# A three-block network on one core: the residual's update at the end of the hybrid mixer, on VectorE alone instead of with GpSimd

## The chip, the core and the metric

The kernel runs on one core of a Trainium2 chip. TensorE does the matrix products and the transposes, VectorE and ScalarE the elementwise work, GpSimd a little of it, and the SyncE queue issues the loads. The metric is the device time of one execution in microseconds.

## What is computed

The input is one sequence of 256 tokens with 1024 columns. It goes through a forgetting-attention layer and a retention layer, each followed by a SwiGLU feed-forward, then a norm, and then through a second block. The second block is the one that matters here:

```python
def second_block(x, ...):
    h = rms_norm(x, attn_pre_norm)
    mix = hybrid_mixer(h, ...)                 # two attentions side by side, then @ w_out
    x = x + rms_norm(mix, attn_post_norm)      # the residual's update
    h = rms_norm(x, ffn_pre_norm)              # the next norm
    f = (silu(h @ w_gate) * (h @ w_up)) @ w_down
    x = x + rms_norm(f, ffn_post_norm)
```

Every number is float32. The large products are made of three products of split numbers: an operand is kept as a high part H and a low part L = x - H.

## The kernel before

The residual lies in one tile `XR` (the profile calls it `xg`, after the tensor that it was loaded into), the tokens on the partitions in two token tiles of 128 at this point of the program. `self.xn(t, hf)` is half `hf` (512 columns) of token tile `t`. The weights come as a stream of granules: `gran` loads one into `raw`, ScalarE makes its high part `wh` (line 221), VectorE its low part `wl` (line 222), and TensorE multiplies. `take` runs up to six granules ahead. A scheduler fixes the order of the instructions on each engine, and each engine works strictly in that order.

The hybrid mixer ends like this. Four heads of the differential attention (`diff_head`: scores on TensorE at lines 1211 and 1212, row maxima with the mask on VectorE at line 1114, exponentials on ScalarE at line 1116) run after the last heads of the other attention (`nsa_head`: transposes at lines 1146 and 1150, values at line 1159). Products of the output projection fill TensorE between them. Then `done(t, banks)` of `post_prep` takes the two PSUM banks of a token tile: `post_norm` squares and sums them on ScalarE (line 318), scales them on VectorE (line 495), and GpSimd raises the sum to the power -1/2 (line 325).

What the next stage needs is `h` transposed and split into `XH` and `XL` (both in the tile `xt`; `split`: H on ScalarE at line 249, L on VectorE at line 250). The kernel before gets it without waiting for the new residual. While the heads still run, GpSimd prepares `xg[t] = X[t] * g` for both token tiles (line 1263, a tile with the same name `xg` in the profile) and `gpg = gp * g` (line 1265), where `gp` is the weight of the norm after the mixer and `g` that of the next norm. Then the split's input is `bank * gpg * r + xg` (lines 495 and 514). The residual itself follows on the side: `add = bank * r * gp` on VectorE (line 516) and `X += add` on GpSimd in `late()` (line 530), after which ScalarE squares it for the next norm (line 318).

The next stage is `ffn` with its first gate chunk (`gate`, Silu on ScalarE at line 616), first for token tile 0 and then for token tile 1; its first products are those of lines 228 to 230, `acc<-wh,xt`.

Of the kernel before, what the change touches and what calls it, by code (L numbers as in the profile page):

```python
# [69 lines left out]
def tiles(w, nk):  # L70
    """w, 1024 rows: granules of nk K tiles each, K on the partitions."""
    return w.reshape(8 // nk, nk, 128, -1).transpose(0, 2, 1, 3).reshape(8 // nk, 128, -1)


def column_tiles(chunks):
    """Granules of 128 x 1024 (or less) of each chunk of columns."""
    out = []
    for parts in chunks:
        w = [m[:, c:c + n] for m, c, n in parts]
        w = np.concatenate(w, axis=1) if len(w) > 1 else w[0]  # L80
        out.append(tiles(w, 4 if w.shape[1] == 256 else 2))
    return np.ascontiguousarray(np.concatenate(out, axis=0))


def row_tiles(w):
    """For each 128 columns of w all its rows, K tile by K tile."""
    return np.ascontiguousarray(w.reshape(-1, 128, 8, 128).transpose(2, 1, 0, 3).reshape(8, 128, -1))


def chunks(w, *cols):  # L90
    """512 columns each from cols; (c,) stands for two chunks of 256."""
    out = []
    for c in cols:
        out += [[(w, c[0], 256)], [(w, c[0] + 256, 256)]] if isinstance(c, tuple) else [[(w, c, 512)]]
    return out


def layout(inputs):
    """The inputs (and constants of the shapes) as the kernel reads them: moved, never computed with."""
# [39 lines left out]
class Net:  # L139
# [48 lines left out]
    def plan(self, src, nk):  # L188
        """Queue granules (nk K tiles each) for take(), in the order of their use."""
        self.queue += [(src[i], nk) for i in range(src.shape[0])]  # L190

    def xn(self, t, hf):
        """The 512 columns hf of token tile t of the residual, while its tokens lie on the partitions."""
        return self.XR[:, 4 * hf:4 * hf + 4, t * 128:(t + 1) * 128]
# [10 lines left out]
    def take(self, hold=0):  # L205
        """The next granule, as (H, L); hold earlier ones are still to be read.  Loads run ahead of it."""
        n = self.taken
        while self.queue and self.made < n - hold + (2 if n < 8 else WBUFS):
            self.ready.append(self.gran(*self.queue.pop(0)))
            self.made += 1  # L210
        self.taken += 1
        return self.ready.pop(0)
# [19 lines left out]
    def run_after(self, fill, then):  # L232
        """then(), its products behind those of the next step of fill, if there is one."""
# [6 lines left out]
    def mm_wide(self, ps, H, L, x, first, last):  # L240
        """ps[:, 0] + ps[:, 1] += H.T @ x[:, 0] + H.T @ x[:, 1] + L.T @ x[:, 0], x = (H, L) side by side."""
# [10 lines left out]
    def xs_part(self, ps, t, i, g):  # L252
        """Adds granule g, two K tiles from 2 i on, of h @ W for the tokens of tile t."""
# [6 lines left out]
    def xs(self, n):  # L260
        """n columns of h @ W, tokens on the partitions: the first token tile as early as it can be."""
# [8 lines left out]
    def xs_steps(self, n, then):  # L270
        """The same granule by granule, for both token tiles; then(t, bank) at the end."""
# [13 lines left out]
    def ws_wide(self, late=False, between=None):  # L285
        """256 columns of h @ W with the columns on the partitions: of each 128 the two addends [128, 2, S]."""
# [12 lines left out]
    def ws(self, between=None):  # L299
        """256 columns of h @ W as two tiles with the columns on the partitions."""  # L300
# [27 lines left out]
    def means(self, acc):  # L328
        """[128, 2] in PSUM: the mean square of each token, for the two token tiles."""
# [11 lines left out]
    def norm(self):  # L341
        """r[t] = 1 / rms of the transposed residual."""
# [5 lines left out]
    def norm_twice(self):  # L348
        """r[t] as of norm() for X = (residual * gf) / rms; returns that 1 / rms, [128, 2]."""
# [14 lines left out]
    def to_rows(self, t, hf, r):  # L364
        """Turns a quarter of the residual, scaled by r, to tokens on the partitions."""
# [5 lines left out]
    def rows(self, cols):  # L371
        """[128, 256] with the two token tiles' columns along every partition."""
# [6 lines left out]
    def out_part(self, bank, g, x, t, hf, first, last):  # L379
        """Adds one K tile, x = (H, L) with K on the partitions, to half hf of the columns of token tile t."""  # L380
# [6 lines left out]
    def out_proj(self, n, lhs, done):  # L387
        """X-side product with K on lhs(k) -> (H, L); done(t, [bank, bank]) takes each token tile."""
# [20 lines left out]
    def out_T(self, nk, lhs, ahead, cut, done):  # L409
        """The residual's transposed update, 128 columns after 128 columns; done(d, bank) takes the two addends  # L410
        of each."""
# [27 lines left out]
    def add_out(self, d, ps):  # L439
        """Adds the update, times scale (one number for each token) if there is one, to the residual."""  # L440
# [10 lines left out]
    def add_T(self, i):  # L451
        """Residual and the split of its norm with the gain i, but for the factor of each token."""
# [17 lines left out]
    def add_norm_T(self, i, f):  # L470
        """The same for a norm with the gain f ahead of it: the residual is left times f."""
# [11 lines left out]
    def post_norm(self, t, banks, g, scaled, f=None):  # L483
        """scaled[hf] = bank * f * g; returns 1 / rms of the rows of the two banks times f."""
# [18 lines left out]
    def post_prep(self, gp, gpg, xg):  # L503
        """X += norm(banks) * gp, and the split of its norm; xg[t] = X[t] * g and gpg = gp * g."""
        nc = self.nc

        def done(t, banks):
            pg = [self.half_tile("pg") for hf in range(2)]
            add = [self.half_tile("add") for hf in range(2)]
            r = self.post_norm(t, banks, gpg, pg)  # L510
            for hf in range(2):
                ks = slice(4 * hf, 4 * hf + 4)
                v = pg[hf].rearrange("p (k n) -> p k n", k=4)
                nc.vector.scalar_tensor_tensor(v, v, r, xg[t][:, ks, :], op0=OP.mult, op1=OP.add)
            for hf in range(2):
                nc.vector.scalar_tensor_tensor(add[hf], banks[hf], r, gp[:, hf * 512:(hf + 1) * 512], op0=OP.mult,
                                               op1=OP.mult)

            def late():
# [8 lines left out]
                for hf in range(2):  # L528
                    x = self.xn(t, hf)
                    nc.gpsimd.tensor_add(x, x, add[hf].rearrange("p (k n) -> p k n", k=4))  # L530
                    self.sumsq(x, a[:, hf:hf + 1])
# [15 lines left out]
    def start_T(self):  # L547
        """The first norm, from x already transposed, and the first chunk of columns."""
# [56 lines left out]
    def ffn(self, done=None, out=None):  # L605
        """done: of the transposed product; out: of the other, the norm's input then being the other as well."""
# [284 lines left out]
    def hybrid(self, gp, gn):  # L891
# [3 lines left out]
        with ExitStack() as st:  # L895
# [23 lines left out]
            def rope(outs, ps, c, s, n):  # L919
                """ps, and each of outs: [128, n, 64] (or [128, a, b, 64])."""  # L920
# [43 lines left out]
            def head_rope_T(t, ps, c, s):  # L964
                """[128 (two heads, d), 4, 128 tokens] of ps, token tile t of 512 columns."""
# [10 lines left out]
            def compressed(i):  # L976
                """The flattened blocks (plus positions), features on the partitions: H and L side by side."""
# [70 lines left out]
            def stack(tr, t):  # L1048
                """Per head H on its own half of the partitions and L on the other half."""
# [126 lines left out]
            def d_evac(i, t, ps):  # L1176
                """Token tile t of the chunk of the differential q, k or v."""
# [82 lines left out]
            xg = []  # L1260
            for t in range(2):
                xg.append(b4("xg", 8, 128))
                nc.gpsimd.tensor_mul(xg[t], self.XR[:, :, t * 128:(t + 1) * 128],
                                     gn.rearrange("p (k n) -> p k n", k=8))
            nc.gpsimd.tensor_mul(gn, gn, gp)
            done = self.post_prep(gp, gn, xg)
# [145 lines left out]
```

## Time and profile before

| | |
|---|---|
| median of three runs | 1050.95 us (1050.90 to 1051.66) |
| span of the profiled execution | 1051.4 us |
| TensorE busy | 1025.1 us, 98% |
| VectorE busy | 739.8 us, 70% |
| ScalarE busy | 568.4 us, 54% |
| GpSimd busy | 32.1 us, 3%, 37 instructions |

The span is that of one execution taken with the profiler, and the three times are of runs without it. They lie around the span, so the time outside the span is no larger than the scatter of the runs. A busy share says how long an engine had work; it does not say whether somebody waited for that work.

### The profile page before, as it was taken

To read this page: it belongs to the slowest core of one execution; us is meant where nothing else is said; L and a number is where in the kernel's file an instruction comes from. 1 tells how busy PE (TensorE), PEld (TensorE's weight loads), DVE (VectorE), ACT (ScalarE), POOL (GpSimd) and SP (SyncE) were. 2 spreads that over 40 slices of the span, in tenths; PEclk is the share of its full clock that TensorE was granted. 3 is DMA by queue.
4 is the path that set the end of the run, shared out by engine and by line. 5 is a ranking of instruction groups with operands and counts; after the bars stand their busy time and mean duration, and the time that the engine had idled before them with its cause. 6 is when DMAs were issued, how large, how long until landed. Compare 5 with 4: busy or idle time off the path is not lost.

```text
span 1051.4 us, 15380 instructions
## 1 busy us (share of the span) xinstructions
PE 1025.1 (98%) x5798; PEld 878.4 (84%) x5798; DVE 739.8 (70%) x1243; ACT 568.4 (54%) x914; POOL 32.1 (3%) x37
## 2 busy tenths in 40 slices
PE   7999999999999999999999999999998989999997
PEld 6999888888889888888888888888776768888885
DVE  6855977676777766767767767778787676776643
ACT  6545666564444354354565655566556655565531
POOL 1000000000000000000000000000003030000000
PEclk9999999999999999999999999999999999999999
DMA  8543755656665455446766566556433046656551
GB/s 273 205 146 116 241 189 181 192 180 184 185 203 178 132 173 186 150 162 199 235 189 184 185 183 190 190 155 216 139 107 101 22 145 215 183 181 197 188 174 40
DMA packets 53386, 181.19 MB, mean 172 GB/s; under 512 B 6833, under 2 KB 8369, under 8 KB 53185
## 3 DMA queue, kind: packets, MB, share of 16 engines
q1 hardware_dynamic: 53280, 180.19, 53.6%
q8 instruction: 45, 0.74, 0.3%
q14 instruction: 29, 0.23, 0.1%
q0 software_dynamic: 32, 0.03, 0.0%
HBM read 179.15 MB, written 1.05 MB: 171 GB/s over the span
## 4 chain that ended last, share of the span: by engine, by line
PE 91%; DVE 3%; DMA 3%; ACT 1%; issue 1%; POOL 1%; DVEq 0%; ACTq 0%; POOLq 0%
PE acc L243 23%; PE acc L244 12%; PE s L243 11%; PE acc L228 10%; PE acc L230 10%; PE acc L229 10%; PE s L244 6%; DVE wl L222 1%; PE o L1159 1%; DMA raw<-in_fox_w_dram 1%; ACT wh L221 1%; DMA raw<-in_hyb_w_dram 1%; PE o L228 1%; PE o L230 1%; PE o L229 1%
## 5 line engine op out<-in xcount | busy, mean ns | idle before, releaser
L222 DVE TENSOR_TENSOR wl<-raw,wh 128x1024 fp32r<-128x1024 f32 (+2 forms) x342 | 410.2, 1203 | 205.1 <-ACT wh L221 204.5
L221 ACT ACTIVATE wh<-raw 128x1024 fp32r<-128x1024 f32 (+2 forms) x342 | 352.3, 1033 | 276.6 <-PE acc L230 61.3
L243 PE MATMUL acc<-xt,wh 128*128 128x512 f32 x496 | 180.7, 398 | 0.0
L243 PE MATMUL s<-xt,wh 128*128 128x512 f32 x496 | 180.6, 397 | 0.0
L244 PE MATMUL acc<-xt,wl 128*128 128x256 f32 x496 | 129.5, 281 | 0.0
L244 PE MATMUL s<-xt,wl 128*128 128x256 f32 x496 | 129.3, 281 | 0.0
L243 PE MATMUL acc<-ht,wh 128*128 128x512 f32 x352 | 122.1, 392 | 0.0
L228 PE MATMUL acc<-wh,xt 128*128 128x512 f32 (+1 forms) x288 | 116.6, 405 | 1.5 <-DVE rm L933 0.9
L230 PE MATMUL acc<-wh,xt 128*128 128x512 f32 (+1 forms) x288 | 115.3, 401 | 2.7 <-DVE xt L250 2.7
L229 PE MATMUL acc<-wl,xt 128*128 128x512 f32 (+1 forms) x288 | 114.0, 396 | 0.0
L243 PEld LDWEIGHTS acc<-xt,wh 128*128 128x128 f32 x496 | 93.3, 188 | 16.8
L243 PEld LDWEIGHTS s<-xt,wh 128*128 128x128 f32 x496 | 93.3, 188 | 16.8
L244 PEld LDWEIGHTS s<-xt,wl 128*128 128x128 f32 x496 | 93.6, 189 | 5.9
L244 PEld LDWEIGHTS acc<-xt,wl 128*128 128x128 f32 x496 | 93.7, 189 | 5.6
L244 PE MATMUL acc<-ht,wl 128*128 128x256 f32 x352 | 96.6, 282 | 0.0
L243 PEld LDWEIGHTS acc<-ht,wh 128*128 128x128 f32 x352 | 65.1, 188 | 13.4
L228 PE MATMUL acc<-xt,wh 128*128 128x256 f32 x256 | 73.2, 286 | 0.0
L230 PE MATMUL acc<-xt,wl 128*128 128x256 f32 x256 | 72.1, 282 | 0.0
L229 PE MATMUL acc<-xt,wh 128*128 128x256 f32 x256 | 72.1, 282 | 0.0
L244 PEld LDWEIGHTS acc<-ht,wl 128*128 128x128 f32 x352 | 66.3, 188 | 1.5
L230 PEld LDWEIGHTS acc<-wh,xt 128*128 128x128 f32 x288 | 55.1, 191 | 14.7 <-DVE xt L250 3.1
L228 PEld LDWEIGHTS acc<-wh,xt 128*128 128x128 f32 x288 | 55.3, 192 | 13.9 <-issue 1.4
(354 smaller groups left out, 1528.9 us busy)
## 6 DMA issues: line engine op xcount, KB each, us to landing
raw<-in_ffn_w_dram SPq DMA_DIRECT2D x132, 512.0 KB, 3.8
raw<-in_ret_w_dram SPq DMA_DIRECT2D x48, 512.0 KB, 3.6
raw<-in_ffn_out_dram SPq DMA_DIRECT2D x32, 512.0 KB, 3.9
raw<-in_w_down_dram SPq DMA_DIRECT2D x22, 512.0 KB, 3.6
raw<-in_fox_w_dram SPq DMA_DIRECT2D x20, 512.0 KB, 4.7
raw<-in_hyb_w_dram SPq DMA_DIRECT2D x20, 512.0 KB, 4.4
raw<-in_ret_out_dram SPq DMA_DIRECT2D x16, 512.0 KB, 4.2
raw<-in_ffn_out_dram SPq DMA_DIRECT2D x16, 384.0 KB, 3.4
```

The costliest lines, as they stand in the source:

```text
L221: nc.scalar.activation(H, w, AF.Copy)
L222: nc.vector.tensor_sub(L, w, H.bitcast(F32))
L228: mm(out, xh, wh, start=first, stop=False, **kw)
L229: mm(out, xh, wl, start=False, stop=False, **kw)
L230: self.last = mm(out, xl, wh, start=False, stop=last, **kw).ins
L243: whole = lambda: mm(ps, H, x, start=first, stop=last).ins
L244: part = lambda: mm(ps[:, 0, :], L, x[:, 0, :], start=False, stop=False).ins
L1159: nc.tensor.matmul(o[hs, t, :], VN[i // 2][:, i % 2, g, :], pt[:, 2 * t + i, :], start=i == 0, stop=i == n - 1)
```

## The change

The residual is updated in place first, `X = (bank * gp) * r + X`, and the split's input is the product `X * g`, both on VectorE. The four products and adds `X += add`, the two products `X[t] * g` and the product `gp * g` on GpSimd are gone, and so are the tiles `xg` and `add`. The square for the next norm is taken of the residual directly. The rest of the diff empties docstrings.

```diff
-    def post_prep(self, gp, gpg, xg):
+    def post_prep(self, gp, g):
         nc = self.nc
 
         def done(t, banks):
             pg = [self.half_tile("pg") for hf in range(2)]
-            add = [self.half_tile("add") for hf in range(2)]
-            r = self.post_norm(t, banks, gpg, pg)
+            r = self.post_norm(t, banks, gp, pg)
             for hf in range(2):
-                ks = slice(4 * hf, 4 * hf + 4)
+                x = self.xn(t, hf)
                 v = pg[hf].rearrange("p (k n) -> p k n", k=4)
-                nc.vector.scalar_tensor_tensor(v, v, r, xg[t][:, ks, :], op0=OP.mult, op1=OP.add)
-            for hf in range(2):
-                nc.vector.scalar_tensor_tensor(add[hf], banks[hf], r, gp[:, hf * 512:(hf + 1) * 512], op0=OP.mult,
-                                               op1=OP.mult)
+                nc.vector.scalar_tensor_tensor(x, v, r, x, op0=OP.mult, op1=OP.add)
+                nc.vector.tensor_mul(v, x, g[:, hf * 512:(hf + 1) * 512].rearrange("p (k n) -> p k n", k=4))
 
             def late():
...
                 for hf in range(2):
-                    x = self.xn(t, hf)
-                    nc.gpsimd.tensor_add(x, x, add[hf].rearrange("p (k n) -> p k n", k=4))
-                    self.sumsq(x, a[:, hf:hf + 1])
+                    self.sumsq(self.xn(t, hf), a[:, hf:hf + 1])
                 self.r[t] = self.rstd(a)
...
-            xg = []
-            for t in range(2):
-                xg.append(b4("xg", 8, 128))
-                nc.gpsimd.tensor_mul(xg[t], self.XR[:, :, t * 128:(t + 1) * 128],
-                                     gn.rearrange("p (k n) -> p k n", k=8))
-            nc.gpsimd.tensor_mul(gn, gn, gp)
-            done = self.post_prep(gp, gn, xg)
+            done = self.post_prep(gp, gn)
```

VectorE's order at the end of the mixer, from the sum of squares of token tile 0 on, before the change (`nv` is the input of the power -1/2, `nf` a factor that only the last norm reads):

```order
L323 SCALAR_TENSOR_TENSOR nv<-na 128x1
L495 TENSOR_TENSOR pg<-acc,gain 128x512
L514 SCALAR_TENSOR_TENSOR pg<-pg,nr,xg 128x512 x2
L516 SCALAR_TENSOR_TENSOR add<-acc,nr,gain 128x512 x2
L222 TENSOR_TENSOR wl<-raw,wh 128x1024 x2
L250 TENSOR_TENSOR xt<-tr,xt 128x4x128 x2
```

and with the change:

```order
L323 SCALAR_TENSOR_TENSOR nv<-na 128x1
L495 TENSOR_TENSOR pg<-acc,gain 128x512
L513 SCALAR_TENSOR_TENSOR xg<-pg,nr,xg 128x4x128 x2
L514 TENSOR_TENSOR pg<-xg,gain 128x512 x2
L222 TENSOR_TENSOR wl<-raw,wh 128x1024 x2
L250 TENSOR_TENSOR xt<-tr,xt 128x4x128 x2
```

There are as many VectorE instructions ahead of the first `xt` as before, but the two that replace `add` now stand between the new residual and the transposes of `pg`. The second token tile has the same exchange.

ScalarE's order from the third granule of the next stage's weights to the first Silu, before the change (the last two lines of `xt` are token tile 1):

```order
L221 ACTIVATE wh<-raw 128x1024
L318 ACTIVATE sq,na<-xg 128x512
L318 ACTIVATE sq,na<-acc 128x512
L318 ACTIVATE sq,na<-s 128x512
L249 ACTIVATE xt<-tr 128x4x128 x2
L318 ACTIVATE sq,na<-xg 128x512
L616 ACT_TABLE_LOAD
L616 ACTIVATE sg<-acc,nr 128x512
```

and with the change:

```order
L221 ACTIVATE wh<-raw 128x1024
L318 ACTIVATE sq,na<-acc 128x512
L221 ACTIVATE wh<-raw 128x1024
L318 ACTIVATE sq,na<-s 128x512
L318 ACTIVATE sq,na<-xg 128x512 x2
L611 ACT_TABLE_LOAD
L611 ACTIVATE sg<-acc,nr 128x512
L249 ACTIVATE xt<-tr 128x4x128 x2
```

The two `xt` of token tile 1 moved behind the table load and the Silu of token tile 0, which read the finished product of token tile 0. On TensorE the eight transposes of token tile 1 moved behind the last product of token tile 0; they stood four products earlier. GpSimd's order only loses the seven instructions, and the order of the loads is unchanged. Up to the end of the heads the order on TensorE, VectorE and ScalarE is the same.

## Rows read from the trace of the kernel before

**Rows 1.** The waits of TensorE over the whole span, two of the longest: who waited for whom, microseconds in total, times, the longest.

```profile
PE s L1211 <- DVE nm L1114: 3.0, 1, 3.0
...
PE acc L230 <- DVE xt L250: 2.7, 1, 2.7
```

**Rows 2.** Two stretches of the span: their length, then busy time (and instructions) of TensorE, its weight loads, VectorE, ScalarE and GpSimd, the granted TensorE clock, the DMA share and GB/s.

```profile
822.00:846.00 24.00, 22.73 (x119) 16.84 (x119) 16.48 (x59) 14.87 (x52) 2.01 (x2) 1.00 0.24 76
867.00:1045.00 178.00, 177.59 (x908) 149.65 (x906) 109.13 (x135) 90.59 (x124) 1.08 (x2) 1.00 0.53 171
```

**Rows 3.** GpSimd's instructions in order of time: start and duration in us (of all merged ones together), line, operation, output and inputs, in brackets the idle time before it and who ended it.

```profile
802.17 4.91 POOL L1263 TENSOR_TENSOR xg<-xg,gain 128x1024 f32<-128x1024 f32 x2 [101.84 <-PE s L1127]
807.16 3.21 POOL L1265 TENSOR_TENSOR gain<-gain 128x1024 f32<-128x1024 f32 x1
...
850.69 3.49 POOL L530 TENSOR_TENSOR xg<-xg,add 128x512 f32<-128x512 f32 x2 [2.19 <-DVE add L516]
```

**Rows 4.** VectorE in order of time among the heads, in the same columns.

```profile
793.81 2.52 DVE L222 TENSOR_TENSOR wl<-raw,wh 128x1024 fp32r<-128x1024 f32 x2
...
803.00 1.84 DVE L250 TENSOR_TENSOR ol<-on,oh 128x256 fp32r<-128x256 f32 x1
804.77 3.39 DVE L222 TENSOR_TENSOR wl<-raw,wh 128x1024 fp32r<-128x1024 f32 x1
...
808.84 1.56 DVE L1138 TENSOR_TENSOR fc<-fc,G 128x4 f32<-128x4 f32 x1
...
813.53 0.16 DVE L1138 TENSOR_TENSOR fc<-fc,G 128x4 f32<-128x4 f32 x1
...
823.43 0.43 DVE L250 TENSOR_TENSOR ol<-on,oh 128x256 fp32r<-128x256 f32 x1 [0.80 <-ACT oh L249]
```

**Rows 5.** TensorE in order of time among the heads. Its matmuls overlap, so the distance of two starts says more than a duration.

```profile
799.90 1.52 PE L1159 MATMUL o<-pt,vn 128*64 128x128 f32 x12
...
805.64 0.39 PE L229 MATMUL acc<-wl,oh 128*128 128x512 f32 x1
809.06 0.46 PE L1211 MATMUL s<-dT 64*128 64x128 f32 x2 [3.03 <-DVE nm L1114]
...
809.88 0.51 PE L230 MATMUL acc<-wh,ol 128*128 128x512 f32 x1
811.35 1.09 PE L1146 MATMUL tr<-c,pr 128*128 128x128 f32 x4 [0.97 <-DVE pr L1139]
...
815.52 2.77 PE L1159 MATMUL o<-pt,vn 128*64 128x128 f32 x12
...
819.88 1.52 PE L1159 MATMUL o<-pt,vn 128*64 128x128 f32 x12
```

**Rows 6.** ScalarE in order of time: the copy of the transposed weights of the last of those heads.

```profile
818.92 0.60 ACT L1147 ACTIVATE pt<-tr 128x512 f32<-128x512 f32 x1 [2.22 <-PE tr L1146]
```

**Rows 7.** Three stretches, in the columns of Rows 2; the number behind the five engines is the granted TensorE clock (1.00 is 2.4 GHz, 0.50 is 1.2 GHz).

```profile
747.00:749.00 2.00, 2.00 (x6) 1.54 (x5) 1.94 (x8) 1.23 (x2) 0.00 (x0) 0.50 0.57 154
814.00:816.00 2.00, 2.00 (x6) 0.98 (x5) 1.52 (x6) 0.78 (x4) 0.00 (x0) 0.50 0.00 0
26.00:28.00 2.00, 2.00 (x19) 2.00 (x18) 0.67 (x2) 2.00 (x3) 0.00 (x0) 1.00 0.87 297
```

**Rows 8.** TensorE at the hand-over from the mixer to the feed-forward: the transposes of `pg` of token tile 0, the first products of the next stage, and two of its products later.

```profile
850.86 1.03 PE L525 MATMUL tr<-c,pg 128*128 128x128 f32 x8
852.48 0.50 PE L228 MATMUL acc<-wh,xt 128*128 128x512 f32 x1 [0.59 <-ACT xt L249]
...
855.92 0.80 PE L230 MATMUL acc<-wh,xt 128*128 128x512 f32 x1 [2.70 <-DVE xt L250]
...
864.38 0.40 PE L230 MATMUL acc<-wh,xt 128*128 128x512 f32 x1
864.62 0.39 PE L228 MATMUL acc<-wh,xt 128*128 128x512 f32 x1
```

**Rows 9.** VectorE at the hand-over, token tile 0.

```profile
848.54 1.41 DVE L514 SCALAR_TENSOR_TENSOR pg<-pg,nr,xg 128x512 f32<-128x512 f32 x2
...
851.19 4.08 DVE L222 TENSOR_TENSOR wl<-raw,wh 128x1024 fp32r<-128x1024 f32 x2
```

**Rows 10.** A VectorE operation of the same kind as the new product (two inputs in SBUF, 512 columns), from the mixer's start: times it occurs, shortest, median and longest duration in ns, first and last start.

```profile
L935 DVE TENSOR_TENSOR nat<-nat,rm x6: 679/684/693, 735.7 to 786.5; 128x512 f32<-128x512 f32 x6
```

**Rows 11.** ScalarE at the hand-over: the high parts of token tile 1 and the first Silu with its table load.

```profile
862.28 1.27 ACT L249 ACTIVATE xt<-tr 128x512 fp32r<-128x512 f32 x2 [5.76 <-PE tr L525]
...
864.17 1.28 ACT L616 ACT_TABLE_LOAD   x1
865.47 0.69 ACT L616 ACTIVATE sg<-acc,nr 128x512 f32<-128x512 f32 x1
```

**Rows 12.** Three stretches at the hand-over, in the columns of Rows 2.

```profile
854.00:856.00 2.00, 0.08 (x1) 0.09 (x1) 2.00 (x3) 1.94 (x6) 0.18 (x1) 0.92 0.69 242
856.00:858.00 2.00, 2.00 (x5) 1.61 (x6) 2.00 (x4) 0.52 (x2) 0.26 (x1) 0.50 0.73 207
858.00:860.00 2.00, 2.00 (x7) 1.54 (x7) 1.95 (x5) 0.00 (x0) 0.83 (x2) 0.73 0.72 160
```

**Rows 13.** TensorE at another wait, earlier in the mixer.

```profile
745.12 0.51 PE L1126 MATMUL s<-KTH,QS 128*128 128x512 f32 x1 [1.84 <-DVE QS L1054]
```

**Rows 14.** TensorE at a wait near the start of the program.

```profile
25.14 0.43 PE L375 MATMUL tr<-c,nr 128*128 128x128 f32 x2 [1.19 <-POOL nr L338]
```

## The prediction

> **What bounds the kernel now.** I read the waits of TensorE first. It is the busiest engine, and two of its three longest waits lie near the change: 3.0 us for a VectorE row-maximum instruction among the heads, and 2.7 us for VectorE's low part at the hand-over to the feed-forward [rows 1]. Then I asked which parts of the span only TensorE paces. From 867 to 1045 us it is busy 177.59 of 178 us, and from 822 to 846 us 22.73 of 24 [rows 2]. What happens earlier only shifts these stretches, so time saved at the two waits should reach the end of the span. Last I read the four engines in order of time around the waits. The reader is to see that both times GpSimd is at work, and that the VectorE instruction ahead of the wait is slow just then.
>
> **Among the heads: what the removed GpSimd products cost.** GpSimd works on its three products from 802.17 to 807.08 and from 807.16 to 810.37 [rows 3]. In that time three VectorE instructions are slow [rows 4]: a low part of 256 columns takes 1.84 us (0.43 later), a weight's low part 3.39 (1.26 as the mean of two before), and a product on 4 columns 1.56 (0.16 later). That last one ends at 810.40, when GpSimd ends. The excess is 1.41 + 2.13 + 1.40 = 4.94 us. GpSimd is idle for long before and after, and I take its work to be the cause. The Trainium skill, SBUF — State Buffer, "Who interferes with whom", says the same of a VectorE instruction with two SBUF inputs beside a GpSimd one that reads SBUF: the later of the two is held up entirely until the other is done. By that rule GpSimd's products also cost VectorE whole waits rather than a share of speed; the trace agrees in the 1.56 us.
>
> Step one is the 3.03 us wait. TensorE's last product before it starts at 805.64 and the next at 809.06 [rows 5]. Products of this size start 0.23 us apart (864.38 and 864.62 [rows 8]), so it could go on at 805.87. The row maximum that it waits for stands behind the first two slow instructions, so it comes 3.5 us sooner, near 805.4. That is early enough: TensorE gains 809.06 - 805.87 = 3.2 us.
>
> Step two is the wait at 811.35, of 0.97 us, for a product that stands behind all three slow instructions. It ends 4.9 us sooner, near 806.3. TensorE comes there 0.82 + 0.23 = 1.05 us after its start at 809.06 (809.88 is the last product between [rows 5]), which is now 806.9. The gain so far is 811.35 - 806.9 = 4.4 us.
>
> Step three is the clock. After the long idle stretch TensorE runs at 1.2 GHz, 0.50 in the stretch from 814 to 816 [rows 7]. Twelve value products take 2.77 us there and 1.52 at the full clock [rows 5], a factor of 0.55. From 811.35 to the last head's value products at 819.88 it needs 8.53 us; 0.55 of this is 4.7. ScalarE must still copy the transposes: 0.60 us for the first copy, and 0.96 us from its start to the products [rows 6, 5]. I lay the transposes' end at 810.85, and the products at 811.75 instead of 819.88. If the idle stretch is gone, I expect the full clock. Steps one to three then give **8.1 us**. The bounds: 4.4 if the clock falls nevertheless, 8.5 if nothing waits at all, and nothing if GpSimd was not the cause. I take 8.1 because the full clock holds from 822 to 846 with the same kinds of work and two short waits [rows 2].
>
> **At the hand-over, token tile 0.** VectorE's four instructions ahead of the weights' low parts are two of the old kind, 1.41 us, and two that I exchange [rows 9]: `add` from PSUM is replaced by a product with both inputs in SBUF. The nearest row for it is 684 ns [rows 10], against 0.7 us each for the ones removed; the strided output of the in-place update has no row, and I set it at nothing (at most 0.1 us, since the old one reads strided operands elsewhere at the same speed). The weights' low parts begin at 851.1 instead of 851.19. There they take 4.08 us for two [rows 9] while GpSimd adds from 850.69 to 854.18 [rows 3]. Without GpSimd two take 2.4 to 2.5 us (2.52 [rows 4]). TensorE goes on 0.65 us after their end (855.27 to 855.92 [rows 8, 9]), so at 854.05 instead of 855.92: 1.9 us sooner. The longer way to the transposes is hidden: the second product ends near 851.2, and TensorE, busy with the other token tile until 850.86, reaches the second four of its eight transposes (1.03 us together) near 851.4 [rows 8].
>
> **At the hand-over, token tile 1: a new wait.** In the new order ScalarE does the table load and the Silu of token tile 0 before the high parts of token tile 1, and the Silu needs the whole product of tile 0. Behind those high parts stands TensorE's first product of tile 1, and behind it the stage. From 854.05 there are 22 products of 0.23 to 0.24 us, to 859.2, then eight transposes to about 860.6 (VectorE's product for the second four is ready near 860.0). ScalarE has finished the squares near 859.55; 1.28 us of table load, 0.6 for the Silu and 0.6 for the first high part [rows 11] end at 862.05. TensorE idles about 1.45 us here, where it had no wait before. Four products later is the one that started at 864.38 [rows 8]; it now starts near 863.0. So of the 1.9 us **1.4** are left. Bounds: 1.9 if the wait is hidden, and a loss of 1.8 if the clock falls twice (below).
>
> **The rest costs nothing.** Weight loads keep their order; they are freed by VectorE's and ScalarE's work, which comes earlier too. The 0.5 us power on GpSimd stays.
>
> **Sum.** 8.1 + 1.4 = 9.5 us. The profiled execution's 1051.4 becomes 1041.9. The median of the runs is 0.45 below that span, so I forecast **1041.5 us**.
>
> **The rivals.**
>
> *The clock falls at the hand-over.* Two idle stretches remain there, about 1.2 us (852.85 to 854.05) and 1.45 us. The rows around waits of that size disagree: after 1.84 us [rows 13] the clock is 0.50 from 747 on [rows 7], after 1.19 us near the start [rows 14] it stays at 1.00 from 26 on [rows 7]. Before the change the hand-over ran 0.32 + 2 + 1.08 = 3.4 us at half the clock (shares 0.92, 0.50, 0.73 [rows 12]), which is 1.7 us lost. A fall at tile 0 delays the end of its product and with it the Silu, so it takes all of the 1.4 and 0.2 more: 1043.1 us. A second one at tile 1 adds 1.7: 1044.8. Both waits are nearer to 1.19 than to 1.84, so I forecast no fall. The Trainium skill, TensorE: Matmul & The Clock Gate, "A second HAM failure mode: psum-queue depth-cycling", speaks for this rival: short, repeated idling between groups of products is enough to make the clock go down and up again. By that rule it falls at both places, 1044.8 us.
>
> *Among the heads the clock stays down.* Only the 4.4 us come: with 1.4 this is 1045.1 us. Against it: no wait of any size is left there.
>
> *The slow VectorE instructions have another cause.* Then nothing changes among the heads. The hand-over's slow pair would have it too, and only the new wait is left: between 1050 and 1051 us, no change. The coincidence of three starts and ends with GpSimd's speaks against it. The same time comes out if a weight load takes the shift back between 822 and 1045; against it, TensorE has next to no idle time there.
>
> *Slower: the new wait at token tile 1.* If ScalarE came to the high parts of tile 1 later than I think, every microsecond is one of TensorE's. The kernel as a whole gets slower by over 0.2% only from a wait of 1.45 + 9.5 + 2.1 = 13 us on, or, if the heads return nothing, of 5 us: 1053 us. In front of the high parts stand 1.28 + 0.69 us of known work, and the product that this waits for ends before the transposes that TensorE does anyway. That is far from either.
>
> **How the numbers follow.** Forecast 0.50; the clock falls at the hand-over 0.30; it stays down among the heads 0.10; no gain among the heads or the shift taken back 0.07; slower 0.03. The range takes in the first three: low 1040.2 (8.5 and 1.9 with some tenths for the starts), high 1045.5. Runs of this kernel differ by 0.07%, and 0.2% (2.1 us) is about what a measurement can tell from no change. The first three cases are faster by more than that: 0.90; same 0.07; slower 0.03.
>
> **What would show it.** Right: the wait on line 1114's result among the heads is gone, low parts of 1024 columns take 1.2 us there, the clock is 1.00 from 805 to 820 on the old scale, and the head's last value products come 8 us sooner. At the hand-over the two low parts take 2.5 us, TensorE's wait for L250 is about 1.2 us, and a new wait of about 1.5 us stands behind the Silu. Wrong: 0.50 in any stretch there, a VectorE instruction that is slow without GpSimd, or the shift of 822 not found at 1045.

## The result and the profile after

The changed kernel takes **1041.02 us** (median of four, 1039.83 to 1042.91). The kernel before takes 1051.31 (median of four) beside it on the same chip. The ratio is 0.9903, with an interval of [0.9889, 0.9918]: 8.6 to 11.7 us are gained. The forecast was 1041.5 in a range of 1040.2 to 1045.5, and the measured time lies in it. The span of the profiled execution is 1039.6 us, its own time 1041.37.

Every run gives its time and its span. In the runs of the kernel before, 2.5 us of the time lie outside the span (59 runs, 2.46 to 2.59), in those of the changed kernel 1.8 (9 runs, 1.74 to 1.83). So about 0.7 of the 10.3 us gained lie outside the span, and no run here shows why. The sentence ahead of the prediction that the time outside the span is no larger than the scatter does not hold: the profiled execution of 1051.4 us was a long one, and two later ones of the same kernel have spans of 1049.3 and 1048.9.

The engines' busy time on the page:

```profile
PE 1022.5 (98%) x5798; PEld 876.8 (84%) x5798; DVE 733.0 (71%) x1243; ACT 568.6 (55%) x914; POOL 19.8 (2%) x30
```

TensorE's longest waits, in the columns of [rows 1]:

```profile
PE s L568 <- DVE fs L250: 5.4, 1, 5.4
PE acc L228 <- ACT xt L249: 1.8, 2, 1.5
PE acc L230 <- DVE xt L250: 1.2, 1, 1.2
```

The 3.0 us for the row maximum are gone, the 2.7 us for VectorE's low part have become 1.2, and a wait of 1.5 us for ScalarE's high part is new. L568 belongs to the start of the program. Line numbers are smaller than before: L1109, L1133, L1154 and L1206 are now what L1114, L1138, L1159 and L1211 were.

VectorE among the heads, the three instructions of [rows 4]:

```profile
800.27 0.42 DVE L250 TENSOR_TENSOR ol<-on,oh 128x256 fp32r<-128x256 f32 x1
800.61 1.22 DVE L222 TENSOR_TENSOR wl<-raw,wh 128x1024 fp32r<-128x1024 f32 x1
...
802.50 0.16 DVE L1133 TENSOR_TENSOR fc<-fc,G 128x4 f32<-128x4 f32 x1
```

TensorE in the same place (to [rows 5]):

```profile
798.62 0.50 PE L1122 MATMUL s<-KTL,QS 128*128 128x512 f32 x1
...
803.23 0.49 PE L1206 MATMUL s<-dT 64*128 64x128 f32 x2
...
804.42 0.60 PE L1141 MATMUL tr<-c,pr 128*128 128x128 f32 x4
...
809.79 1.52 PE L1154 MATMUL o<-pt,vn 128*64 128x128 f32 x12
```

The stretch that answers to 814 to 816 of [rows 7]:

```profile
804.00:806.00 2.00, 2.00 (x12) 1.37 (x11) 0.74 (x8) 1.43 (x5) 0.00 (x0) 1.00 0.40 154
```

The slow three of 1.84, 3.39 and 1.56 us take 0.42, 1.22 and 0.16. TensorE goes through without a wait, at 2.4 GHz (granted clock 1.00).

TensorE at the hand-over (to [rows 8]):

```profile
840.77 1.07 PE L522 MATMUL tr<-c,pg 128*128 128x128 f32 x8
842.05 0.50 PE L228 MATMUL acc<-wh,xt 128*128 128x512 f32 x1 [0.22 <-ACT xt L249]
...
843.99 0.50 PE L230 MATMUL acc<-wh,xt 128*128 128x512 f32 x1 [1.21 <-DVE xt L250]
...
849.23 1.22 PE L522 MATMUL tr<-c,pg 128*128 128x128 f32 x8
852.00 0.50 PE L228 MATMUL acc<-wh,xt 128*128 128x512 f32 x1 [1.54 <-ACT xt L249]
...
853.04 0.40 PE L230 MATMUL acc<-wh,xt 128*128 128x512 f32 x1
```

VectorE's low parts of the weights (to [rows 9]) and ScalarE ahead of tile 1 (to [rows 11]):

```profile
840.98 2.36 DVE L222 TENSOR_TENSOR wl<-raw,wh 128x1024 fp32r<-128x1024 f32 x2
...
849.47 1.28 ACT L611 ACT_TABLE_LOAD   x1
850.77 0.69 ACT L611 ACTIVATE sg<-acc,nr 128x512 f32<-128x512 f32 x1
851.35 1.08 ACT L249 ACTIVATE xt<-tr 128x512 fp32r<-128x512 f32 x2
```

The two stretches in which TensorE idled (to [rows 12]):

```profile
842.00:844.00 2.00, 0.74 (x3) 0.31 (x3) 2.00 (x4) 2.00 (x6) 0.00 (x0) 1.00 0.44 41
850.00:852.00 2.00, 0.46 (x5) 0.22 (x3) 1.13 (x4) 1.99 (x4) 1.29 (x1) 1.00 0.41 94
```

Both waits are there, about as long as forecast (1.2 and 1.45), and the clock keeps its 1.00 through both.

**Where the span went.** Four marks cut the span so that kernels can be compared stretch by stretch: TensorE's first L1122 product among the heads (L1127 before), the value products of the last of those heads, the last Silu of the feed-forward, and TensorE's last product. The rows of before that stand for the first, third and fourth:

```profile
801.35 0.50 PE L1127 MATMUL s<-KTL,QS 128*128 128x512 f32 x1
...
979.55 0.63 ACT L645 ACTIVATE sg<-sg 128x512 f32<-128x512 f32 x1 [0.59 <-DVE sg L644]
...
1044.19 0.39 PE L230 MATMUL o<-wh,ht 128*128 128x512 f32 x1
```

All kernels of this study, in us (each stretch from one profiled execution; the time is the median of its own runs). They ran in groups on different chips. The kernel before took 1051.31 beside after, 1050.53 beside e1 to e4, 1052.01 beside a2, e5 and e6, 1050.11 beside e7 and e8, and 1050.16 beside b2 and b3; times of different groups are compared through the ratio to it, which is given with each run:

| kernel | time | start to heads | heads | hand-over to last Silu | to last product |
|---|---|---|---|---|---|
| before | 1051.31 | 801.35 | 18.53 | 159.67 | 64.64 |
| b2_before | 1051.30 | 799.45 | 18.43 | 159.60 | 64.65 |
| b3_before | 1051.42 | 798.31 | 18.94 | 159.78 | 64.66 |
| after | 1041.02 | 798.62 | 11.17 | 158.40 | 64.65 |
| a2_after | 1040.36 | 797.55 | 11.17 | 158.37 | 64.65 |
| e1_products_back | 1048.40 | 797.25 | 18.98 | 158.37 | 64.65 |
| e2_no_products | 1042.15 | 797.84 | 11.16 | 159.83 | 64.65 |
| e3_one_product | 1040.92 | 796.49 | 12.06 | 158.35 | 64.65 |
| e4_gp_memsets | 1040.20 | 798.66 | 11.17 | 158.40 | 64.65 |
| e5_early_silu | 1038.84 | 797.23 | 11.16 | 157.14 | 63.14 |
| e6_order | 1038.54 | 798.84 | 11.16 | 156.40 | 63.14 |
| e7_tile_copy | 1040.47 | 800.30 | 11.16 | 158.40 | 63.14 |
| e8_silu_no_tile | 1038.60 | 798.38 | 11.17 | 157.08 | 64.65 |

From before to after the heads lose 18.53 - 11.17 = 7.36 us and the way from there to the last Silu 159.67 - 158.40 = 1.27, together 8.6. The spans differ by 11.8. Of the rest 2.73 us lie ahead of the heads, where the order of TensorE, VectorE and ScalarE did not change; two runs below are on that.

### The profile page after: what moved, and what is told of

Read it like the earlier page. It is cut to its first block, busy times and chain, and to the rows that moved or that the text cites. A ratio compares the mean times of both kernels' runs of the same rounds, so it can differ in the third digit from the quotient of the medians.

```text
span 1039.6 us, 15367 instructions
## 1 busy us (share of the span) xinstructions
PE 1022.5 (98%) x5798; PEld 876.8 (84%) x5798; DVE 733.0 (71%) x1243; ACT 568.6 (55%) x914; POOL 19.8 (2%) x30
## 4 chain that ended last, share of the span: by engine, by line
PE 95%; DVE 2%; DMA 1%; ACT 1%; issue 1%; POOL 0%; DVEq 0%; ACTq 0%; POOLq 0%
PE acc L243 23%; PE acc L244 12%; PE s L243 11%; PE acc L228 11%; PE acc L230 11%; PE acc L229 11%; PE s L244 6%; PE o L1154 1%; DVE wl L222 1%; PE o L228 1%; PE o L230 1%; PE o L229 1%; DMA raw<-in_hyb_w_dram 0%; DMA raw<-in_v_w_dram 0%; PE tr L845 0%
```

## The experiments

My theory (Theory 1 in the texts): GpSimd's products, which read SBUF, hold up VectorE instructions with two SBUF inputs. Among the heads this makes two TensorE waits, and behind them the clock falls to half. The hand-over gives a small part of its own.

### The three products put back into the changed kernel

```diff
+            xg = []
+            for t in range(2):
+                xg.append(b4("xg", 8, 128))
+                nc.gpsimd.tensor_mul(xg[t], self.XR[:, :, t * 128:(t + 1) * 128], ...)
+            gpg = self.late.tile([128, DM], F32, name="gpg", bufs=1)
+            nc.gpsimd.tensor_mul(gpg, xg[1].rearrange("p k n -> p (k n)"), gp)
             done = self.post_prep(gp, gn)
```

> The changed kernel with three GpSimd products of the old sizes put back among the heads (two of the residual by the weight, one of the same length after them); nobody reads their results. Theory 1 (GpSimd holds VectorE up there, TensorE waits, its clock falls): the heads lose what they had gained, 7.4 to 8.1 us, so 1048 to 1049.5 us; TensorE again waits about 3 us for line 1109, and the low part of 1024 columns takes about 3.4 us. Theory 2 (the gain among the heads comes from somewhere else: other tiles, weights that arrive at another time): as fast as the changed kernel, 1040 to 1042 us.

Measured: 1048.4 us, ratio to before 0.998 [0.9971, 0.999]. GpSimd's products, VectorE and TensorE in its trace, in order of time:

```profile
798.06 4.91 POOL L1258 TENSOR_TENSOR xg<-xg,gain 128x1024 f32<-128x1024 f32 x2 [99.24 <-PE s L1122]
...
798.90 1.84 DVE L250 TENSOR_TENSOR ol<-on,oh 128x256 fp32r<-128x256 f32 x1
800.66 3.39 DVE L222 TENSOR_TENSOR wl<-raw,wh 128x1024 fp32r<-128x1024 f32 x1
...
804.95 0.77 PE L1206 MATMUL s<-dT 64*128 64x128 f32 x2 [3.03 <-DVE nm L1109]
```

A stretch behind that wait, in the columns of [rows 2]:

```profile
808.00:810.00 2.00, 2.00 (x8) 1.28 (x6) 0.78 (x6) 1.80 (x8) 0.00 (x0) 0.50 0.03 8
```

The products alone bring back the slow instructions to the hundredth of a microsecond, the wait of 3.03 us and the clock of 0.50. They cost 7.8 us in the trace (18.98 against 11.17). In the times it is 8.2 against the kernel with memsets below, which ran beside it (1048.40 and 1040.20). What stays of the gain is 2.1 us (1.1 to 3.0). The hand-over's 1.3 us in the trace and the 0.7 us outside the span (1.8 here too) make up that size.

### The products alone taken out of the kernel before

```diff
-            xg = []
-            for t in range(2):
-                xg.append(b4("xg", 8, 128))
-                nc.gpsimd.tensor_mul(xg[t], ...)
-            nc.gpsimd.tensor_mul(gn, gn, gp)
+            xg = [self.XR[:, :, t * 128:(t + 1) * 128] for t in range(2)]
             done = self.post_prep(gp, gn, xg)
```

> The kernel before with the three GpSimd products among the heads left out: the residual itself stands in for X * g, and the weight g for gp * g, so the outputs lack a factor; every other instruction stays, the GpSimd adds at the hand-over too. Theory 1: 7.4 to 8.1 us faster than before, 1043 to 1044 us; the hand-over keeps its wait of 2.7 us. Theory 2: no change among the heads, 1050 to 1052 us.

Measured: 1042.15 us, ratio 0.9926 [0.9909, 0.9944], so 5.9 to 9.6 us gained. Its hand-over keeps the adds and the `add` tiles of before; TensorE's wait there:

```profile
PE acc L230 <- DVE xt L250: 2.8, 1, 2.8
```

The stretch behind it, with the granted clock of 0.54:

```profile
846.00:848.00 2.00, 2.00 (x7) 1.58 (x6) 2.00 (x5) 0.00 (x0) 0.98 (x2) 0.54 0.66 244
```

The heads are as short as in after (11.16 us). The hand-over shows the long wait of before and the fallen clock, and takes 1.43 us more than in after. So in the traces the two parts of the change add up, and each is seen alone. VectorE's two weight low parts at the hand-over take 4.13 us here beside GpSimd's adds, 4.08 before and 2.36 in after. But no run took the adds alone away and left VectorE's order as it was, so at the hand-over the adds as the cause are argued from the same pattern and not shown.

### One product of the three, or GpSimd work that only writes

The first run keeps the first product alone:

```diff
+            xg = b4("xg", 8, 128)
+            nc.gpsimd.tensor_mul(xg, self.XR[:, :, 0:128], gn.rearrange("p (k n) -> p k n", k=8))
             done = self.post_prep(gp, gn)
```

> The changed kernel with only the first of the three GpSimd products put back, its result unread. It holds up one VectorE instruction by 1.4 us, of which 0.5 us are hidden behind TensorE's products. If the price is a wait plus a fall of the clock that only a long wait brings: 0.9 us slower than the changed kernel, about 1042, clock 1.00 among the heads. If the price is in proportion to GpSimd's work: about 2.6 us, 1043.6.

The second puts eight memsets of 128x1024 in the products' place, so that GpSimd is as long at work but reads nothing:

```diff
+            for t in range(2):
+                xg = b4("xg", 8, 128)
+                for i in range(4):
+                    nc.gpsimd.memset(xg, float(i))
             done = self.post_prep(gp, gn)
```

> The changed kernel with eight GpSimd memsets of 1024 columns in the place of the products, about 8 us of GpSimd that writes SBUF and reads nothing. If only GpSimd's reads stand in VectorE's way (the Trainium skill, SBUF - State Buffer, says so of a VectorE instruction with two inputs in SBUF): no VectorE instruction is slower, 1040 to 1042 us as the changed kernel. If any GpSimd work there holds VectorE up: 1048 to 1049.5 us.

Measured: 1040.92 us (0.9907 [0.9891, 0.9922]) with one product, 1040.2 us (0.9901 [0.9885, 0.9918]) with the memsets. The one product beside VectorE and TensorE:

```profile
797.30 2.39 POOL L1256 TENSOR_TENSOR xg<-xg,gain 128x1024 f32<-128x1024 f32 x1 [97.74 <-PE s L1122]
...
798.14 1.84 DVE L250 TENSOR_TENSOR ol<-on,oh 128x256 fp32r<-128x256 f32 x1
799.90 1.21 DVE L222 TENSOR_TENSOR wl<-raw,wh 128x1024 fp32r<-128x1024 f32 x1
...
802.01 0.46 PE L1206 MATMUL s<-dT 64*128 64x128 f32 x2 [0.85 <-DVE fc L1133]
```

The memsets beside the same two VectorE instructions:

```profile
799.46 7.45 POOL L1258 MEMSET xg<- 128x1024 f32 x8 [99.61 <-PE s L1122]
...
800.31 0.42 DVE L250 TENSOR_TENSOR ol<-on,oh 128x256 fp32r<-128x256 f32 x1
800.65 1.22 DVE L222 TENSOR_TENSOR wl<-raw,wh 128x1024 fp32r<-128x1024 f32 x1
```

One product holds up one VectorE instruction, until it ends at 799.69; the next one runs at full speed. TensorE waits 0.85 us, keeps its clock, and loses 12.06 - 11.17 = 0.9 us. A third of GpSimd's work costs an eighth of the 7.4 us, so the price is not in proportion to GpSimd's time: it sits in the length of TensorE's wait and in the clock. The timed median cannot tell 0.9 us from nothing, so this rests on the trace.

The memsets keep GpSimd busy for 7.45 us and cost VectorE nothing. The Trainium skill, SBUF — State Buffer, "Who interferes with whom", says that a VectorE instruction with two SBUF inputs contends with GpSimd instructions that read SBUF, and not with those that only write. The two runs agree with both halves (1.84 us beside a product, 0.42 beside memsets).

### The new wait at the hand-over: an early Silu, and another order

Three kernels ran beside each other on one chip: the changed kernel again, one with a small Silu ahead of the last differential norm, so that ScalarE loads its table there, and that one with three weight granules moved behind the work that TensorE waits for.

> The changed kernel once more, as the yardstick for the two kernels beside it: 1041.0 us, 10 us under the kernel before. Among the heads TensorE should again show no wait on VectorE's row maximum, with 11.2 us from the product of the first L1122 there to the last L1154. The 2.7 us by which the changed kernel's profiled execution came earlier to the heads already is, by my theory, an accident of a weight load in the execution of before and no part of the change: then this execution may show a wait of some 1.8 us ahead of the heads (as before did at 745), or none, with the same distances behind it. If it were of the change, the heads would again begin 2.7 us earlier than in the kernel before.

Measured: 1040.36 us, 0.9896 [0.9881, 0.991]. Same heads, same hand-over (table above). It came to the heads at 797.55 us with no wait for `QS` ahead of them, which leaves both readings open; two runs of the kernel before, further down, go on from there.

```diff
                 nc.vector.tensor_scalar(a, a, EPS, None, op0=OP.add)
+                if last:
+                    nc.scalar.activation(self.sm.tile([128, 1], F32, name="early"), a[:, 0:1], AF.Silu)
...
```

The lines that are cut pass `last`, which is true for the second of the two norms.

> The changed kernel with one small Silu more, of 128x1, ahead of the last differential-attention norm, so that ScalarE loads its table before the hand-over. Theory (TensorE's new wait of 1.54 us before tile 1's first product is the table load of 1.28 us on ScalarE's path to the high parts): that wait falls to 0.2 to 0.3 us, the product that started at 853.04 comes 1.3 us sooner, 1039.7 us. If ScalarE waits at that place for the product of tile 0 or for the squares anyway, the wait of 1.5 us stays: 1041 us. If the early load is on the path of the differential norm, it costs up to 1.3 us there: 1041 us too, with the wait at the hand-over gone.

Measured: 1038.84 us, 0.9871 [0.9856, 0.9885]. The table load lies elsewhere, and the wait of 1.54 us is 0.25:

```profile
829.32 1.28 ACT L1243 ACT_TABLE_LOAD   x1
...
849.34 0.50 PE L228 MATMUL acc<-wh,xt 128*128 128x512 f32 x1 [0.25 <-ACT xt L249]
```

That is 1.26 us in the trace (158.40 to 157.14), as expected: the load was on the path of the new wait with its whole length. But the last stretch also fell, from 64.65 to 63.14 us, which no theory had foreseen.

```diff
+        with ExitStack() as st:
+            for ins in self.behind.pop(0) if self.behind else ():
+                st.enter_context(self.tc.issue_after(ins))
             nc.scalar.activation(H, w, AF.Copy)
             nc.vector.tensor_sub(L, w, H.bitcast(F32))
...
+                if not t:
+                    self.behind += [[], [m.ins]]
...
+            if t:
+                self.behind += [[m.ins], [m.ins, self.sq]]
```

Here `m` is the last low part of tile 0's transposes in the first list, and tile 1's product with the gain in the second; `self.sq` is tile 1's last square.

> The kernel of e5 with the order at the hand-over changed too: the low parts of the feed-forward's second granule of weights stand behind the low parts of tile 0's transposes, those of the third and fourth behind tile 1's product with the gain. Theory (the 1.21 us wait of TensorE for tile 0's low parts is VectorE's two weight low parts of 1.2 us each in front of them): that wait falls to some 0.1 us, and tile 1's norm comes up to 1.2 us sooner: together with e5's part 2.0 to 2.6 us under the changed kernel, 1038.4 to 1039.0. Rival (VectorE's and ScalarE's whole work at the hand-over is the bound, whatever its order): TensorE then waits as long a little later, for the weights' low parts that were put back, and the time is that of e5 within 0.4 us.

Measured: 1038.54 us, 0.9868 [0.9854, 0.9882]. What is left of TensorE's waits at the hand-over (L528 are the transposes of tile 1, L530 their high parts):

```profile
PE tr L528 <- DVE pg L518: 0.5, 1, 0.5
...
PE acc L232 <- ACT xt L530: 0.2, 1, 0.2
```

The 1.21 us for tile 0's low part is gone and 0.45 us came back at the transposes of tile 1. The trace shows 0.74 us beyond e5 (157.14 to 156.40), between theory (1.2) and rival (under 0.4). The times of e5 and e6 cannot be told apart.

### What shortened the last stretch

Two kernels separate the early table load from the small tile that its result needs. Their diffs are shown against the kernel of e5.

```diff
-                    nc.scalar.activation(self.sm.tile([128, 1], F32, name="early"), a[:, 0:1], AF.Silu)
+                    nc.scalar.activation(self.sm.tile([128, 1], F32, name="early"), a[:, 0:1], AF.Copy)
```

> The run of the early Silu showed a second gain that nobody had asked for: from the last Silu of the feed-forward to TensorE's last product 63.14 us instead of the 64.65 of six other kernels. This run has the changed kernel with the same small tile of 128x1, but a Copy by ScalarE in place of the Silu, so no table load is moved. Theory (the tile's place in SBUF moves the feed-forward's buffers, and the last stage's products start a little closer to each other): 63.14 us again, 1.5 us under the changed kernel, 1039.3, with TensorE's wait of 1.54 us before tile 1 as it was. Rival (the earlier table load, or the state of ScalarE, does it): 64.65 us and 1041.

```diff
-                    nc.scalar.activation(self.sm.tile([128, 1], F32, name="early"), a[:, 0:1], AF.Silu)
+                    nc.scalar.activation(on[:, 3, 127:128], a[:, 0:1], AF.Silu)
```

> The early Silu without a tile of its own: it writes into a column that is overwritten right behind it. Theory (table load and tile are two separate gains): TensorE's wait before tile 1's first product falls from 1.54 to 0.25 us, and from the last Silu of the feed-forward to the last product it takes 64.65 us as before: 1.3 us under the changed kernel, 1039.5. Rival (the last stage's gain comes from the early table load): 63.14 us there, 1038.2.

Measured: 1040.47 us (0.9899 [0.9884, 0.9915]) with the tile and a Copy, 1038.6 (0.9891 [0.9875, 0.9907]) with the Silu and no tile. A stretch of the last stage with the tile (TensorE's busy time and its number of products come first):

```profile
995.00:1015.00 20.00, 20.00 (x90) 16.57 (x89) 8.58 (x7) 8.05 (x8) 0.00 (x0) 1.00 0.49 159
```

The same stretch without it:

```profile
995.00:1015.00 20.00, 20.00 (x87) 16.20 (x86) 8.57 (x7) 7.45 (x8) 0.00 (x0) 1.00 0.42 134
```

Without the tile TensorE's wait at tile 1 is 0.26 us and the hand-over is as short as in e5. (The scheduler gave this kernel another order at tile 0: the wait for tile 0's low parts is 0.20 us there, and 0.83 us of waiting for `pg` stand ahead of its transposes.) With the tile and no Silu the wait is 1.54 us and the last stretch 63.14. So these are two separate effects: the table load costs 1.3 us at the hand-over, and with the tile the last stage is 1.5 us shorter, at the same granted clock, by products that start closer together. All three kernels with the tile show it and all seven others do not. Why is open: the tile may have moved buffers that are laid out after it, but no run varied the place alone. In the times the tile's 1.5 us are not settled. By the ratios e7 (0.9899) is level with a2 (0.9896), and its profiled execution came to the heads latest of all those with the changed code; e5 (0.9871) lies 2 us under e8 (0.9891), but their intervals overlap. The tile as the cause thus rests on the traces alone.

### The kernel before, profiled again

> The kernel before, unchanged, to settle 2.7 us of the span that no step explains: its profiled execution came to the heads (first product of L1127 there) at 801.35 us, the others at 796.5 to 800.3. Theory (an accident of one execution): it comes there at 796.5 to 800.3 this time, with the heads at 18.5 us and hand-over to last Silu at 159.7; its span is then some 1048 to 1050 us. Rival (the old code, or where its tiles lie, is later ahead of the heads too): again at 801 or later, and 1.5 to 2.7 us of the measured gain of 10.3 come from ahead of the heads.

> The same once more, for a third profiled execution of the kernel before: at the heads between 796.5 and 800.3 us if the 801.35 was an accident, at 801 or later if it belongs to this kernel.

Measured: 1051.3 us, ratio of the same kernel to itself 1.0014 [0.9997, 1.0031], and one execution of 1051.42. The spans are 1049.3 and 1048.9 us, and the heads begin at 799.45 and 798.31. So the 801.35 was the late end of a scatter, and the heads and the hand-over are as in the first profile. A part of the scatter has a place: TensorE's wait for `QS` ahead of the heads. In the first of the two:

```profile
PE s L1126 <- DVE QS L1054: 1.7, 1, 1.7
```

In the second:

```profile
PE s L1126 <- DVE QS L1054: 0.6, 1, 0.6
```

In the first profile it was 1.84 us [rows 13], and none in the two executions of the changed kernel. It is not the whole scatter: e7 came to the heads at 800.30 us without this wait. The three executions of before come there at 799.7 us in the mean, the two of after at 798.1. With e2, whose code ahead of the heads is the old one, the old kernel's four have a mean of 799.2; the nine executions with the changed code ahead of the heads have 798.1 and reach from 796.5 to 800.3. Whether the 1 to 1.6 us between them are chance or belong to the old kernel stays open. With the 0.7 us outside the span they would account for the difference between the 8.6 us of the trace and the 10.3 of the times.

## Why the prediction was right, point by point

**GpSimd as the cause.** Among the heads it is shown, by e1 and e2 from both sides; e4 shows that it is GpSimd's reading and not its being busy. At the hand-over it is argued from the same pattern.

**Step one**, 3.2 us: from the first L1127 to the row maximum's customer it took 7.71 us (801.35 to 809.06 [rows 5]), now 4.61 (798.62 to 803.23). That is 3.10.

**Step two**, 4.4 us in sum: 10.00 us to 811.35 [rows 5], now 5.80 to 804.42. That is 4.20.

**Step three**, 8.1 us in sum: 7.36 measured. The mechanism held (clock 1.00 all through) and the factor did too, but the length it was applied to was too long. I took 0.55 of all 8.53 us up to the last value products. The clock had come back earlier than that, as two stretches of before show (columns of [rows 2]):

```profile
816.00:818.00 2.00, 2.00 (x11) 1.94 (x10) 1.26 (x8) 0.60 (x2) 0.00 (x0) 0.50 0.00 0
818.00:820.00 2.00, 2.00 (x15) 1.28 (x14) 0.34 (x1) 0.87 (x2) 0.00 (x0) 0.97 0.00 0
```

The first piece of TensorE's work there at the full clock:

```profile
818.23 0.66 PE L1146 MATMUL tr<-c,pr 128*128 128x128 f32 x4
```

From 818.23 to 819.88 before took 1.65 us, and the same pieces take 1.65 in after (808.14 to 809.79). Only the 6.88 us from 811.35 to 818.23 shrank, to 3.72 (804.42 to 808.14), a factor of 0.54. Step three is therefore 3.16 us, not 3.7. I had read the clock in one stretch of two microseconds [rows 7], and not to its end.

**The hand-over**, 1.4 us: from the transposes of tile 0 to the product at 864.38 [rows 8] it took 13.52 us, now 12.27 (840.77 to 853.04). That is 1.25. The two weight low parts take 2.36 us (I said 2.5), the wait for tile 0 is 1.21 (1.2), and the new wait behind table load and Silu is 1.54 (1.45). e5 and e8 show that the table load is what it hangs on: without it 0.25 and 0.26 us are left.

**The sum** was 9.5; the trace gives 7.36 + 1.27 = 8.6, and the times 10.3 (8.6 to 11.7). On the mechanisms the forecast was a microsecond too hopeful. That it lies within half a microsecond of the median is in part luck: about 0.7 us were gained outside the span and about 1 us ahead of the heads, and no step named either. The base was luck too: the 0.45 us between span and median compared a long execution with the times of shorter ones, while in each run of before the time is 2.5 us longer than its own span.

**The rivals.** The clock did not fall at the hand-over, neither after 1.21 us of idle time nor after 1.54. The rule that I had set beside it (the Trainium skill, TensorE: Matmul & The Clock Gate, "A second HAM failure mode: psum-queue depth-cycling") would have put 1044.8 us here; this trace does not bear it out, 1.00 in every stretch from 838 to 858. In e2, where the wait is 2.76 us, the clock does fall behind it. The row of 1.84 us with the fallen clock, which I had weighed against that of 1.19, was no firm guide: in b2 the same product waited 1.74 us, and the clock kept its 1.00:

```profile
744.78 0.50 PE L1126 MATMUL s<-KTH,QS 128*128 128x512 f32 x1 [1.74 <-DVE QS L1054]
...
746.00:748.00 2.00, 2.00 (x10) 1.64 (x10) 1.91 (x5) 1.28 (x2) 0.00 (x0) 1.00 0.19 25
```

Nor did the clock stay down among the heads. The gain was not taken back later: from the last Silu on, before and after differ by 0.01 us. The slower case did not come. One price among the rivals does not add up: with another cause of the slow instructions the new wait would have come on top of 1050.95 us, by the prediction's own terms some 0.5 us (1.9 less 1.4), and not between 1050 and 1051; nothing that was measured rests on it.

## What to carry to other kernels

When a VectorE instruction with two SBUF inputs is several times slower than its twin elsewhere, look whether GpSimd reads SBUF at that moment. Moving a few microseconds of elementwise work from GpSimd to VectorE can be worth more than VectorE then pays for it. What was paid here was the stall, what waited behind it, and TensorE's clock after it. Price a stretch at the lower clock only as far as the stretches of the profile show that clock. A change that takes a wait away often hands it on to the next late thing in the queue, here ScalarE's table load, and that one is cheap to move.

## What was not expected of the hardware

**GpSimd is held up in the other direction.** Its power on 128x1 takes 0.55 us alone. It takes 1.46 when it starts while VectorE is at a weight's low part, an instruction with two SBUF inputs, which ends at 845.73 (after, in order of time):

```profile
837.86 0.55 POOL L325 TENSOR_TENSOR nr<-nv,mhalf 128x1 f32<-128x1 f32 x1 [6.53 <-DVE nv L323]
...
844.51 1.22 DVE L222 TENSOR_TENSOR wl<-raw,wh 128x1024 fp32r<-128x1024 f32 x1
844.68 1.46 POOL L325 TENSOR_TENSOR nr<-nv,mhalf 128x1 f32<-128x1 f32 x1 [6.27 <-DVE nv L323]
```

TensorE does not wait for it here. I had said that this power stays at 0.5 us. The third GpSimd product of before may be the same thing: it took 3.21 us against 2.46 as the mean of the two ahead of it [rows 3], and it started while VectorE's slow low part still ran [rows 4].

**The clock fell without a wait of TensorE.** In after it was 0.50 from 760 to 762, ahead of the heads, with TensorE busy for all of it, behind a series of products of only 16 columns. In before it was 1.00 around that place and 0.50 earlier, at 747 [rows 7]; in e3 and e5 it fell at neither. In the other ten executions, of the old code and the new, it fell somewhere between 756 and 769, so this is no part of the change. What decides it is open, and it may be part of the scatter ahead of the heads. The stretch with the fallen clock in after:

```profile
760.00:762.00 2.00, 2.00 (x7) 1.38 (x7) 2.00 (x6) 0.37 (x1) 0.00 (x0) 0.50 0.37 152
```

**With one tile of 128x1 more, a stage 150 us later ran at another pace**, by 1.5 of 64.65 us, as told above; the reason is open.
